# Block 1's FFN: gate and up products with the tokens stationary, their result transposed on TensorE

## The chip, the core and the metric

The kernel runs on one core of one Trainium2 chip. The metric is the device time of one launch in microseconds (us). The profile is of one execution of the same program, taken by the hardware profiler; its times are us from the start of that execution's span, and PE stands for TensorE, DVE for VectorE, ACT for ScalarE, POOL for GpSimd and SP for SyncE.

## What is computed

Two transformer blocks on 256 tokens of width 2048, in float32. Block 1 has a mixer, a cross attention and a gated FFN; block 2 a mixer with pooling and an FFN. The change is in block 1's FFN and in the hand-over to it:

```python
x = x + rms_norm(o @ w_co[l], cross_post_g[l])          # end of the cross attention

h = rms_norm(x, ffn_pre_g[l])
gate, up = jnp.split(h @ w_ffn_in[l], 2, axis=-1)       # 2048 -> 2 x 5632
x = x + rms_norm((jax.nn.silu(gate) * up) @ w_ffn_out[l], ffn_post_g[l])   # 5632 -> 2048
```

`rms_norm` divides each token by the root of its mean square and multiplies by a gain per column.

## The kernel before

**Weights.** All weights come as one stream of halves, 128 x 1024 numbers (512 KB) in the order of use, loaded ahead by SP's queue (L175) into five buffers. Each half is split into `h`, which TensorE takes exactly in a single pass, and the exact rest `l`: ACT copies to `h` (L199), DVE subtracts to `l` (L200; POOL for a few halves). Five buffers hold `h` and `l` of five halves; normally `stream.half()` splits the half that comes four after the one now used. Activations are split in the same way into a `Pair`: for each tile of 128 features the high parts of 256 tokens and then the low parts. A product is `h*H + h*L + l*H`, all three summed in one PSUM accumulator.

**Two forms of product.** `cols` (L349) has the weights stationary: for a tile of 128 weight columns, and each of the 16 k-tiles, one instruction streams the 256 high parts and 256 low parts of the tokens past `h` (512 columns, L379), another the 256 high parts past `l` (L378, for the first k-tile L381). It leaves out^T, features across the partitions, in two halves of a bank that must be added (`sum2`, L475 and L476). `rowsmm` (L397) has the tokens stationary: for 512 weight columns, a token block `tb` of 128 tokens and each k-tile, three instructions of 512 columns (L423 to L425); a half holds two k-tiles, so it takes 12 of these for both token blocks. It leaves tokens across the partitions.

**Accumulators.** `acc()` gives one of three PSUM banks, `bank()` one of five others for transposes and small products.

**Around the products.** Each engine takes its instructions in the order in which the program emits them. `self.later(f)` leaves `f` for the `settle()` after the next half's products; `tick()` runs a step of waiting side work.

**Block 1's FFN** (`ffn`, L1454). The 5632 hidden columns are cut into parts of 8, 8, 8, 8, 4, 8 tiles of 128 (`FFN_PARTS`, 44 tiles). Step `i0` makes part 0 of the hidden values, `o0` multiplies it with its rows of `w_ffn_out`; the order is i0 i1 o0 i2 o1 i3 o2 i4 o3 i5 o4 o5. The i steps use `cols` on tiles of gate and up in turn (32 halves for a part of 8), the o steps `rowsmm` (16 halves). In an i step each tile is added (ACT, DVE), multiplied with `rbx` (L1472), which is 1/rms of each token laid out along the free axis, the same in every partition; a gate tile goes through Silu (L1474), an up tile is multiplied with it (L1477) and split into the Pair `hid` (L468, L469). In o0 the result is copied by ACT (L1490), in o1 to o4 added by DVE (L1492).

**The hand-over.** The cross attention's output product is a `rowsmm` with a chain: its last seven halves run for the first token block and then for the second. Meanwhile the first block's x is updated (`up`, L1180), transposed on TensorE (`tr`, L1218) and split times a gain into the Pair `hT` (`ev`, L1229 on ACT, L1231 on DVE); the last four tiles of `ev` are left for later. After the second token block `after1` makes that block's scale (L1154 and L508 to L512), updates x, has PE run five products of nothing (`warm`, L634), finishes two postponed products with the gain (`finish`, L817), and lays the remaining updates, transposes and splits of the second block, two tiles at a time, between the k-tiles of the first tile of `i0` (`self.pre`). Three halves of weights are split ahead. `stats_gen` makes 1/rms of x and `rbx` beside the next products; the first evictions wait for it.

Of the kernel before, what the change touches and what calls it, by code (L numbers as in the profile page):

```python
# [15 lines left out]
AF = mybir.ActivationFunctionType  # L16
# [25 lines left out]
# ---------------------------------------------------------------- host layout  # L42

def _cols(w):
    """K x N -> per tile of 128 columns, [128 (k in tile), K/128, 128]; K 2048 or 1024."""
    k, n = w.shape
    t = w.reshape(k // 128, 128, n // 128, 128).transpose(2, 1, 0, 3)
    if k == 1024:
        t = t.reshape(n // 256, 2, 128, 8, 128).transpose(0, 2, 1, 3, 4)
    return t.reshape(-1, 128, 2048)  # L50


def _rows(w, n0=0, n1=None):
    """K x N -> per block of 512 columns and 512 rows, [128 (k in tile), 4, 512]."""
    k, n = w.shape
    t = w.reshape(k // 512, 4, 128, n // 512, 512).transpose(3, 0, 2, 1, 4)
    return t.reshape(-1, 128, 2048)


def _weights(a):  # L60
# [13 lines left out]
    gate_up = np.stack([_cols(w_fi[:, :FFN]), _cols(w_fi[:, FFN:])], axis=1).reshape(-1, 128, 2048)  # L74
    starts = np.cumsum((0,) + FFN_PARTS)
    for step in FFN_ORDER:
        p = int(step[1:])
        lo, hi = int(starts[p]), int(starts[p + 1])
        u.append(gate_up[2 * lo:2 * hi] if step[0] == "i" else _rows(w_fo[lo * 128:hi * 128]))
# [70 lines left out]
# ---------------------------------------------------------------- the program  # L150

class Stream:
    """The weights in the order of use, in halves of 128 x 1024: loaded ahead and split into a part
    that the tensor engine's single pass carries exactly and the exact remainder."""
# [14 lines left out]
    def loading(self):  # L169
        """the load of the next half; the very first one in two pieces."""  # L170
# [43 lines left out]
class Pair:  # L214
    """An operand [128 (k in tile), nkt, 256 tokens], split into two parts side by side; 4 k-tiles per slot."""
# [18 lines left out]
class Chain:  # L234
    """What rowsmm does besides: before all of it, after[tb] after the first and the second block of tokens,
    at[i] before the last but i half of the second; the weights that come next are split ahead of the
    second block (ahead) and after its halves in splits."""
# [6 lines left out]
class Prog:  # L244
# [22 lines left out]
    # -- tiles  # L267
# [32 lines left out]
    # -- work that runs beside the products  # L300
    def tick(self):
        """one step of each waiting piece of work, as far as the vector engine has time beside a unit of
        weights; what a generator yields is the cost of its next step there."""
# [33 lines left out]
    def finish(self):  # L337
        """what ev_post leaves for after the start of the chain."""
        last, self.last = self.last, []
        for f in last:  # L340
            f()
# [6 lines left out]
    # -- products  # L348
    def cols(self, xp, nkt, ntiles, evac, ready=None, wide=0, wider=False):  # L349
        """out^T tile j [128 columns, 256 tokens] for each tile of weight columns; with wider, in two halves  # L350
        of a bank that evac has to add (the second: what the low parts of xp give). The first tiles
        (wide) go through the first half of k together. What evac needs may not be there yet: then
        up to four tiles wait until it is (ready)."""
# [42 lines left out]

    def rowsmm(self, xp, nkt, ncb, evac, chain=None, lead=7):  # L397
        """out [128 tokens, 512 columns] for each block of columns and of tokens. With a chain, the last
        halves (lead) are done for the first block of tokens before the second, so that what
        follows the first (chain) runs beside the second."""  # L400
# [35 lines left out]
        for i in range(n):  # L436
# [28 lines left out]
    # -- small pieces  # L465
    def split2(self, v, h, l):
        """h + l = v exactly, h in the tensor engine's single-pass form."""
# [3 lines left out]
    def sum2(self, out, ps):  # L471
        """the two halves that cols leaves."""
# [10 lines left out]
    def split_later(self, v, h, l):  # L483
        """split2, left for after the next products' weights: neither engine waits for the other then."""
# [6 lines left out]
    def rsqrt(self, v, n, scale, eps, y=None):  # L491
        """1 / sqrt(v * scale + eps) of a small tile: the scalar engine's root, inverted, and a Newton step."""
# [11 lines left out]
    def rsqrt2(self, v, scale, eps, name="r"):  # L504
        """rsqrt of [128, 1], in fewer steps."""
# [14 lines left out]
    def diag(self, r):  # L520
        """[128 tokens, 2] on the diagonals of two blocks."""
# [5 lines left out]
    def across(self, d, name="rbc"):  # L527
        """diag of r [128 tokens, 2] -> r [128, 256 tokens], the same in every partition."""
# [8 lines left out]
    def row(self, i, name="row"):  # L537
        """row i of the per-column vectors, the same in every partition."""
# [9 lines left out]
    # -- the whole  # L548
# [81 lines left out]
    def warm(self, n):  # L630
        """n products of nothing, for the tensor engine's clock not to drop while it waits."""
# [4 lines left out]
    def norm_gen(self, t, r):  # L636
        """per token: 1 / sqrt(mean square + eps)."""
# [11 lines left out]
    def small_gen(self):  # L649
        """what depends on the small inputs alone."""  # L650
# [8 lines left out]
        # the lower bound of the forget gate: softmax over one layer, its running sum less the first  # L659
# [13 lines left out]
        # the factor of the second softmax map, negated  # L673
# [10 lines left out]
    def bias_gen(self):  # L684
        """bias[q, h, k] of the distance 128 + q - k, with the causal mask."""
# [35 lines left out]
    # ------------------------------------------------------------ block 1: mixer  # L721
# [79 lines left out]
    def ev_post(self, y, g, ss, add=True):  # L801
        """the last part of a product before a post-norm: the sum, its mean square, times the gain."""
# [21 lines left out]
    def da_gen(self, q, k, v, o_pair):  # L824
# [4 lines left out]
        # per head and map: the second block of queries (256 keys), then the first (128)  # L829
# [81 lines left out]
    def head_out(self, o_t, ss, p, g, gate=None):  # L911
        """o [128 tokens, 2, 8 heads, 128]: its rms norm per head (and gate), transposed, times g, split."""
# [24 lines left out]
    def hg_gen(self, fg, qg, rb):  # L937
# [57 lines left out]
        def s0(i):  # L995
# [4 lines left out]
            if lv == 1:  # L1000
                # q * k for the diagonal; one step back the decay is f = 1 - k itself
# [148 lines left out]
    # ------------------------------------------------------------ post-norm, residual, next operand  # L1150
    def rms_of(self, ss, tb):
        """ss [128, 2, 4] of squares -> 1 / sqrt(mean + eps) of one block of tokens."""
# [4 lines left out]
    def moments(self, c, tb, n):  # L1157
        """of x[tb], n columns from c on, for ln_of."""
# [3 lines left out]
    def ln_of(self, tb):  # L1162
        """of one block of tokens: rsqrt(var + eps), the mean, what sets the last, and -mean * rsqrt."""
# [6 lines left out]
    def residual(self, y, ss):  # L1170
        """update for spread: x += y * rsqrt(mean square)."""
# [12 lines left out]
    def layer(self, g, b):  # L1184
        """update for spread: x = (x - mean) * rsqrt(var + eps) * g + b."""
# [22 lines left out]
    def spread(self, update, xp, g=None):  # L1208
        """the pieces of: update x, then xp = the split of x^T * g; for n tiles of 128 columns from k on of
        the block of tokens tb."""  # L1210
# [10 lines left out]
        def ev(tb, k, n):  # L1221
# [5 lines left out]
            # a bank is read by one engine at a time  # L1227
# [8 lines left out]
    def root(self):  # L1236
        """has the scalar engine ready for its root."""
        self.nc.scalar.activation(out=self.junk[:, :1], in_=self.eps[RMS_EPS], func=AF.Sqrt)

    def chain(self, pieces, order, ahead=3, late=False, stats=None):  # L1240
        """for rowsmm: x and xp, of the first block of tokens beside the products of the second, and of
        the second as the next products (cols) go through k."""
# [47 lines left out]
        return Chain(self.root, after0, after1, {i: at(ks) for i, ks in order.items()}, ahead=ahead)  # L1290
# [478 lines left out]
```

## Time and profile before

| | us |
|---|---|
| median of 3 runs | 2638.34 (2636.83 to 2640.91) |
| span of the profiled execution | 2643.8 |
| PE busy in it | 2606.6 |
| DVE busy | 1706.0 |
| ACT busy | 1306.5 |

Busy time of PE is the time in which at least one instruction is under way; they are pipelined, so that the durations of single ones add up to more than the time. The pace of a stream of products is therefore read from the distance of their starts. "Idle before" in a row is the time that the engine stood still ahead of the instruction, and the name behind the arrow is what ended it. The granted clock of TensorE is given as a share of 2.4 GHz.

### The profile page before, as it was taken

The page shows a single profiled execution, that of the slowest core. Times are in us where ns is not written, and L with a number is a line of the kernel's source. Part 1 is how long each engine was busy: PE and PEld are TensorE (multiplying, and loading weights), DVE is VectorE, ACT ScalarE, POOL GpSimd, SP SyncE. Part 2 cuts the span into 40 slices and gives each one's busy share as a digit, 9 for nine tenths or more (in the row PEclk, how much of TensorE's full clock was granted, in tenths as well). Part 3 has the DMA queues.
Part 4 walks back from the last instruction along what each step waited for, and adds up shares of the span by engine and source line. Part 5 has one row for each costly group of instructions (what it writes and reads, how often), then busy time and mean ns, then how long its engine had stood idle before and what let it go on. Part 6 is the DMA issues. An engine that isn't in the chain of part 4 may idle for free. (4 is left out here: it accounts for less than half of the span.)

```text
span 2643.8 us, 37315 instructions
## 1 busy us (share of the span) xinstructions
PE 2606.6 (99%) x14419; PEld 2254.9 (85%) x14422; DVE 1706.0 (65%) x2416; ACT 1306.5 (49%) x1931; POOL 64.7 (2%) x60
## 2 busy tenths in 40 slices
PE   9999999999999999999999999999999999999997
PEld 8989888988888888888878888888788888888886
DVE  5865757767665656556676765577675665665566
ACT  6533666665454444444444455555454444444443
POOL 0000000110000000000010000000100000000001
PEclk9999999999999999999999999999999999999999
DMA  7544557545555555555556645666455555556553
GB/s 278 179 148 138 177 177 247 197 160 172 186 188 188 189 186 190 192 191 191 184 168 196 215 162 173 191 217 193 148 191 189 186 190 192 190 190 220 191 190 118
DMA packets 134098, 493.57 MB, mean 187 GB/s; under 512 B 15149, under 2 KB 15541, under 8 KB 131744
## 3 DMA queue, kind: packets, MB, share of 16 engines
q1 hardware_dynamic: 129888, 470.34, 54.0%
q0 software_dynamic: 2880, 17.76, 2.0%
q10 hardware_dynamic: 1152, 3.07, 0.3%
q8 instruction: 114, 1.87, 0.3%
q14 instruction: 64, 0.52, 0.1%
HBM read 486.91 MB, written 2.11 MB: 185 GB/s over the span
## 5 line engine op out<-in xcount | busy, mean ns | idle before, releaser
L200 DVE TENSOR_TENSOR l<-w,h 128x1024 fp32r<-128x1024 f32 (+1 forms) x880 | 1071.5, 1223 | 672.7 <-ACT h L199 667.8
L199 ACT ACTIVATE h<-w 128x1024 fp32r<-128x1024 f32 (+1 forms) x883 | 926.4, 1056 | 595.2 <-PE pa L425 381.4
L379 PE MATMUL pa<-hT,h 128*128 128x512 f32 x2376 | 829.9, 398 | 0.0
L378 PE MATMUL pa<-hT,l 128*128 128x256 f32 x2228 | 626.3, 281 | 0.0
L379 PEld LDWEIGHTS pa<-hT,h 128*128 128x128 f32 x2376 | 437.5, 188 | 97.8
L378 PEld LDWEIGHTS pa<-hT,l 128*128 128x128 f32 x2228 | 421.1, 189 | 5.7
L423 PE MATMUL pa<-h,hid 128*128 128x512 f32 (+1 forms) x864 | 334.6, 387 | 0.0
L424 PE MATMUL pa<-l,hid 128*128 128x512 f32 (+1 forms) x864 | 334.4, 387 | 0.0
L425 PE MATMUL pa<-h,hid 128*128 128x512 f32 (+1 forms) x864 | 334.4, 387 | 0.0
L379 PE MATMUL pa<-xT,h 128*128 128x512 f32 x872 | 303.8, 397 | 0.0
L475 ACT ACTIVATE sum<-pa 128x256 f32<-128x256 f32 x239 | 92.1, 386 | 358.4 <-PE pa L379 358.2
L378 PE MATMUL pa<-xT,l 128*128 128x256 f32 x818 | 231.2, 283 | 0.0
L424 PEld LDWEIGHTS pa<-l,hid 128*128 128x128 f32 x864 | 162.2, 188 | 33.2
L425 PEld LDWEIGHTS pa<-h,hid 128*128 128x128 f32 x864 | 162.2, 188 | 33.1
L423 PEld LDWEIGHTS pa<-h,hid 128*128 128x128 f32 x864 | 162.3, 188 | 32.7
L379 PEld LDWEIGHTS pa<-xT,h 128*128 128x128 f32 x872 | 160.2, 188 | 34.8
L476 DVE TENSOR_TENSOR sum<-pa,sum 128x256 f32<-128x256 f32 x183 | 77.8, 425 | 137.1 <-ACT sum L475 137.1
L378 PEld LDWEIGHTS pa<-xT,l 128*128 128x128 f32 x818 | 154.5, 189 | 2.4
L383 PE MATMUL pa<-xT,h 128*128 128x256 f32 x496 | 144.4, 291 | 1.4 <-ACT xT L488 1.4
L385 PE MATMUL pa<-xT,l 128*128 128x256 f32 x496 | 142.5, 287 | 0.2 <-DVE l L200 0.2
L384 PE MATMUL pa<-xT,h 128*128 128x256 f32 x496 | 142.5, 287 | 0.1
L423 PE MATMUL pa<-h,xT 128*128 128x512 f32 x256 | 104.2, 407 | 2.6 <-ACT ghg L738 1.4
(449 smaller groups left out, 3186.1 us busy)
## 6 DMA issues: line engine op xcount, KB each, us to landing
w<-W SPq DMA_DIRECT2D x889, 512.0 KB, 3.9
row<-rows POOLq DMA_DIRECT2D x7, 1024.0 KB, 6.4
xn<-x ACTq DMA_DIRECT2D x2, 1024.0 KB, 10.3
mn<-mem POOLq DMA_DIRECT2D x2, 1024.0 KB, 7.2
memraw<-memT POOLq DMA_DIRECT2D x2, 1024.0 KB, 6.7
x<-x POOLq DMA_DIRECT2D x2, 1024.0 KB, 7.4
xraw<-xT SPq DMA_DIRECT2D x3, 512.0 KB, 9.5
out<-x SPq DMA_DIRECT2D x6, 256.0 KB, 2.5
```

Of the source, the lines that this page charges most:

```text
L199: nc.scalar.activation(out=h[:, s], in_=t[:, s], func=AF.Copy)
L200: (nc.gpsimd if j in self.slow else nc.vector).tensor_tensor(l[:, s], t[:, s], h[:, s].bitcast(F32), OP.subtract)
L378: mm(o[:, :S], l[:, k], xp.H(kt), start=False, stop=False)
L379: mm(o, h[:, k], xp.both(kt), start=kt == 0, stop=kt == nkt - 1)
L383: mm(o, h[:, k], xp.H(kt), start=kt == 0, stop=False)
L384: mm(o, h[:, k], xp.L(kt), start=False, stop=False)
L385: mm(o, l[:, k], xp.H(kt), start=False, stop=kt == nkt - 1)
L423: mm(o, xh, h[:, k, c], start=kt == 0, stop=False)
L424: mm(o, xh, l[:, k, c], start=False, stop=False)
L425: mm(o, xl, h[:, k, c], start=False, stop=kt == nkt - 1)
L475: nc.scalar.activation(out=t, in_=ps[:, S:], func=AF.Copy)
L476: nc.vector.tensor_tensor(t if out is None else out, ps[:, :S], t, OP.add)
```

## The change

The i steps of block 1's FFN use `rowsmm`: tokens stationary, 512 gate columns and then the 512 up columns that go with them, which the host lays out in that order. `ev_glu` takes each accumulator with one instruction: Silu of gate times r on ACT, and (up times r) times that on DVE; r, 1/rms per token, is now a scalar per partition, so `rbx` isn't made. The product has tokens across the partitions, so `turn_later` transposes it on TensorE, four tiles of 128 x 128 to a bank, after the next half's products for the first token block and after the one behind that for the second; the split into `hid` reads that bank one half later.

In the hand-over (`lagged`) the warm-up products are gone, the second block's x is updated and transposed four tiles at a time, and `rowsmm` of i0 (`lag=4`) runs its first four halves for the first token block alone and then for the second, with the second block's pieces between them. Halves 3 to 5 are split while the first block's products run, ahead of these pieces in the queues of ACT and DVE.

```diff
-    gate_up = np.stack([_cols(w_fi[:, :FFN]), _cols(w_fi[:, FFN:])], axis=1).reshape(-1, 128, 2048)
+    gate_up = np.stack([_rows(w_fi[:, i:i + FFN]).reshape(-1, 4, 128, 2048) for i in (0, FFN)], axis=1)
...
-        u.append(gate_up[2 * lo:2 * hi] if step[0] == "i" else _rows(w_fo[lo * 128:hi * 128]))
+        u.append(gate_up[lo // 4:hi // 4].reshape(-1, 128, 2048) if step[0] == "i" else _rows(w_fo[lo * 128:hi * 128]))
...
-    def rowsmm(self, xp, nkt, ncb, evac, chain=None, lead=7):
+    def rowsmm(self, xp, nkt, ncb, evac, chain=None, lead=7, lag=0):
...
-        for i in range(n):
+        first = []
+        for tb in range(2 if lag else 0):
+            for i in range(lag):
+                if tb == 0:
+                    first.append(view(stream.half(2)))
+                self.pre.pop((tb, i), lambda: None)()
+                run(*halves[i], first[i], tb)
+                if tb and i % 2:
+                    stream.split()
+                    self.tick()
+        assert not self.pre or not lag
+        for i in range(lag, n):
...
-    def chain(self, pieces, order, ahead=3, late=False, stats=None):
+    def chain(self, pieces, order, ahead=3, late=False, stats=None, lagged=False):
...
-        return Chain(self.root, after0, after1, {i: at(ks) for i, ks in order.items()}, ahead=ahead)
+        def piece(k, more=None):
+            def f():
+                tr(1, k, 4)
+                ev(1, k, 4)
+                if more is not None:
+                    up(1, more, 4)
+                if more == 12 and stats is not None:
+                    self.stats = self.start(self.norm_gen(self.x, stats))
+            return f
+
+        def after1_lagged():
+            prep(1)
+            up(1, 0, 4)
+            up(1, 4, 4)
+            self.finish()
+            if late:
+                ev(0, 12, 4)
+            self.pre = {(0, 2): piece(0, 8), (0, 3): piece(4, 12), (1, 1): piece(8), (1, 3): piece(12)}
+
+        return Chain(self.root, after0, after1_lagged if lagged else after1, {i: at(ks) for i, ks in order.items()}, ahead=ahead)
...
-        self.rowsmm(o_pair, 4, 4, self.ev_post(y, g, ss, add=False), self.chain(self.spread(self.residual(y, ss), self.hT, self.ffn_pre), ORDER, late=True, stats=self.rxx))
+        self.rowsmm(o_pair, 4, 4, self.ev_post(y, g, ss, add=False), self.chain(self.spread(self.residual(y, ss), self.hT, self.ffn_pre), ORDER, late=True, stats=self.rxx, lagged=True))
...
-
-                def ev(j, ps, hp=hid[p]):
-                    t = self.sum2(None, ps)
-                    nc.vector.tensor_tensor(t, t, self.rbx, OP.mult)
-                    if j % 2 == 0:
-                        nc.scalar.activation(out=t, in_=t, func=AF.Silu)
-                        sg[0] = t
-                    else:
-                        nc.vector.tensor_tensor(t, t, sg[0], OP.mult)
-                        self.split_later(t, hp.H(j // 2), hp.L(j // 2))
-
-                self.cols(hT, 16, 2 * nt, ev, self.have_rbx, wider=True)
+                self.rowsmm(hT, 16, nt // 2, self.ev_glu(hid[p]), lag=4 if p == 0 else 0)
...
+    def ev_glu(self, hp):
...
+        def f(c0, tb, ps):
+            r = self.rxx[:, tb:tb + 1]
+            blk, up = divmod(c0 // 512, 2)
+            if not up:
+                self.drain(self.stats)
+                sg[tb] = self.t2([128, 512], "sg")
+                nc.scalar.activation(out=sg[tb], in_=ps, func=AF.Silu, scale=r)
+                return
+            t = sg.pop(tb)
+            nc.vector.scalar_tensor_tensor(out=t, in0=ps, scalar=r, in1=t, op0=OP.mult, op1=OP.mult)
+            self.turn_later(t, hp, 4 * blk, tb)
+        return f
+
+    def turn_later(self, t, hp, k, tb):
...
+        def tr():
+            ps = self.bank()
+            for i in range(4):
+                self.nc.tensor.transpose(ps[:, i * 128:(i + 1) * 128], t[:, i * 128:(i + 1) * 128], self.ident)
+            self.later(lambda: self.split2(
+                ps.rearrange("p (k t) -> p k t", k=4), hp.H(k, 4, tb * 128, tb * 128 + 128), hp.L(k, 4, tb * 128, tb * 128 + 128)))
+
+        def wait():
+            self.later(tr)
+        self.later(wait if tb else tr)
```

## Rows read from the trace of the kernel before

**Rows 1.** The page: span, busy time by engine, and the weights' split on ACT.

```profile
span 2643.8 us, 37315 instructions
PE 2606.6 (99%) x14419; PEld 2254.9 (85%) x14422; DVE 1706.0 (65%) x2416; ACT 1306.5 (49%) x1931; POOL 64.7 (2%) x60
...
L199 ACT ACTIVATE h<-w 128x1024 fp32r<-128x1024 f32 (+1 forms) x883 | 926.4, 1056 | 595.2 <-PE pa L425 381.4
```

**Rows 2.** Busy time by stretch: engines, then granted clock, DMA share, GB/s.

```profile
580.00:590.00 10.00, 10.00 (x65) 8.91 (x63) 9.46 (x28) 5.81 (x21) 2.84 (x2) 1.00 0.58 217
590.00:595.00 5.00, 2.30 (x11) 0.87 (x10) 3.92 (x16) 4.29 (x17) 0.00 (x0) 1.00 0.01 2
595.00:598.40 3.40, 3.35 (x11) 2.80 (x12) 2.14 (x8) 0.62 (x2) 0.00 (x0) 0.50 0.00 0
598.40:607.00 8.60, 8.22 (x48) 6.56 (x47) 5.39 (x16) 6.36 (x17) 0.00 (x0) 1.00 0.01 2
607.00:780.00 173.00, 173.00 (x985) 150.43 (x984) 115.91 (x166) 91.08 (x136) 0.00 (x0) 1.00 0.59 192
```

**Rows 3.** What PE waited for, 590 to 1350 us: total, times, longest.

```profile
PE pa L634 <- ACT junk L518: 3.5, 2, 2.8
PE pa L379 <- DVE hT L1231: 1.8, 2, 1.5
```

**Rows 4.** Timeline of PE: first products of o0, i2, o1, i3, o2.

```profile
780.16 0.39 PE L423 MATMUL pa<-h,hid 128*128 128x512 f32 x1
...
823.68 0.39 PE L379 MATMUL pa<-hT,h 128*128 128x512 f32 x1
...
914.02 0.39 PE L423 MATMUL pa<-h,hid 128*128 128x512 f32 x1
...
957.54 0.39 PE L379 MATMUL pa<-hT,h 128*128 128x512 f32 x1
...
1047.89 0.39 PE L423 MATMUL pa<-h,hid 128*128 128x512 f32 x1
```

**Rows 5.** Timeline of PE: transposes between products; then all transposes of their line.

```profile
584.10 0.60 PE L1218 MATMUL pb<-ident,x 128*128 128x128 f32 x4
584.46 0.48 PE L423 MATMUL pa<-h,ocx 128*128 128x512 f32 x1
584.77 0.40 PE L424 MATMUL pa<-l,ocx 128*128 128x512 f32 x1
...
L1218 PE MATMUL pb<-ident,x x128: 270/273/447, 487.6 to 1921.2; 128*128 128x128 f32 x128
```

**Rows 6.** Timeline of DVE at the end of o2; ACT's evictions in o0.

```profile
1089.98 1.23 DVE L200 TENSOR_TENSOR l<-w,h 128x1024 fp32r<-128x1024 f32 x1 [1.49 <-ACT h L199]
1091.12 1.28 DVE L1492 TENSOR_TENSOR yf<-pa,yf 128x512 f32<-128x512 f32 x2
...
L1490 ACT ACTIVATE yf<-pa x8: 598/599/601, 789.9 to 823.9; 128x512 f32<-128x512 f32 x8
```

**Rows 7.** Timeline of PE: the last product of the cross attention.

```profile
589.99 0.28 PE L425 MATMUL pb<-h,ocx 128*128 128x256 f32 x1
```

**Rows 8.** Timeline of DVE and ACT in the hand-over.

```profile
581.51 3.34 DVE L1180 SCALAR_TENSOR_TENSOR x<-yc,r,x 128x512 f32<-128x512 f32 x4
...
587.95 2.16 DVE L1231 SCALAR_TENSOR_TENSOR hT<-pb,pv,hT 128x128 fp32r<-128x128 f32 x8 [0.22 <-ACT hT L1229]
...
591.27 1.12 ACT L1229 ACTIVATE hT<-pb,pv 128x128 fp32r<-128x128 f32 x4
...
591.90 0.21 DVE L512 TENSOR_SCALAR r<-d,r 128x1 f32<-128x1 f32 x1
...
592.95 0.42 DVE L817 TENSOR_TENSOR yc<-pa,row 128x256 f32<-128x256 f32 x1
...
593.28 0.42 DVE L817 TENSOR_TENSOR yc<-pb,row 128x256 f32<-128x256 f32 x1
...
606.10 4.63 DVE L200 TENSOR_TENSOR l<-w,h 128x1024 fp32r<-128x1024 f32 x4 [1.71 <-ACT h L199]
```

More of the change, by code (lines that the diff above doesn't have):

```diff
@@ L1459, in ffn @@
         hid = {}
-        sg = {}
         g = self.row(2)
@@ L1493, in ffn @@
             self.rowsmm(hid.pop(p), nt, 4, ev)
+    def ev_glu(self, hp):
+        nc = self.nc
+        sg = {}
+        def f(c0, tb, ps):
[20 more added lines that the diff above has]
+        self.later(wait if tb else tr)
     def rope_gen(self, cs):
```

## The prediction

> **What bounds the kernel now.** I read the page's busy table first: TensorE (PE) is busy 2606.6 us of a span of 2643.8 us, DVE 1706.0 us [rows 1]. Then the stretches around block 1's FFN: from 607 to 780 us PE is busy 173.00 of 173.00 us, DVE 115.91 and ACT 91.08, at clock 1.00 [rows 2]. In such a stretch only two things move the time: the pace of PE's own instructions, and a new wait in front of one of them. The exception is the hand-over from the cross attention's output product to the FFN, 590 to 607 us: PE is busy 2.30 of the first 5.00 us, and the 3.4 us after that run at clock 0.50, the lower level of 1.2 GHz, behind the idle time [rows 2]. The waits name what PE waits for there: the squares on ACT whose output the warm-up products read, and the low parts of the second token block on DVE [rows 3]. So I cost three terms: the pace of a half of weights, the new transposes, the hand-over. Whatever shrinks on DVE or ACT inside the FFN is worth nothing by itself.
>
> **Term 1, the pace.** FFN steps i and o alternate, and the first PE instruction of each gives its length [rows 4]. Step i2 runs from 823.68 to 914.02 us, 90.34 us for its 32 halves, 2.823 us each; i3 (957.54 to 1047.89) gives 90.35 us, the same. Steps o0 (780.16 to 823.68) and o1 (914.02 to 957.54) take 43.52 us for 16 halves, 2.720 us each. Both kinds stream the same number of columns per half, 8 x (512 + 256) = 12 x 512 = 6144; the i form does it in 16 instructions, half of them narrow, the o form in 12. The change turns every i half into the o form: the same instruction, 128 tokens stationary and 512 weight columns moving, with hT in the place of hid. FFN_PARTS sums to 44 tiles of hidden columns, twice that for gate and up, two halves each: 176 halves. Gain: 176 x (2.823 - 2.720) = 18.1 us. The order of weights in memory changes, the number of halves, their bytes and their split into h and l do not, so DMA, ACT and DVE pay per half what they pay now.
>
> **Term 2, the transposes.** Eleven blocks of 512 hidden columns, two token blocks each, four transposes of 128x128: 22 groups, 88 instructions, all on PE and so all on the path. The nearest rows are the same transposes between products of the same width: the group at 584.10 us starts the next product at 584.46 and the one after at 584.77 [rows 5]. Without the group the second of these products would have started one product's spacing (2.720 / 12 = 0.227 us) after 584.10; so the group costs 584.77 - 584.10 - 0.227 = 0.443 us, 0.11 us per transpose. (Two more groups in that product, of 8 and of 4, work out to the same 0.11.) Loss: 22 x 0.443 = 9.7 us. Bounds: 0.36 us per group if the following product lost nothing, 7.9 us in all; 4 x 0.273 = 1.09 us if nothing overlapped and each took the full duration of its row [rows 5], 24.0 us in all. I take the spacing, because instructions of PE overlap: the 512-column product has a duration of 0.39 us and a spacing of 0.227.
>
> The Trainium skill (TensorE: Matmul & The Clock Gate, Part 4: PE-mode transpose) gives about 275 ns for a transpose inside a kernel and says that transposes do not count as activity for the clock. The first figure is the duration of the row, not its spacing; by it the sum would be near zero, and that is a rival below. On the second, no row speaks against a full clock: the 10 us with those transposes have clock 1.00 [rows 2].
>
> **Who could make PE wait inside a step.** After the last half of an up block DVE multiplies each token block out of PSUM with the activated gate (new 512-column instruction, nearest row the o-step's eviction at 1091.12 us, 1.28 us for two [rows 6]); the first group of transposes stands behind one more half of products, the second behind two. Counted from the start of that last half, ACT and DVE first split the half that comes four later (ACT 1.06 [rows 1], DVE 1.23 [rows 6]), so DVE is free at about 2.5 us and done with the first block by 3.2 and the second by 3.9; the transposes come at 5.4 and 8.6 us. That is 2 us of cover. The rows agree: DVE's evictions begin at 1091.12 us, right behind its split at 1089.98, with nothing between [rows 6]. On the gate side ACT takes 0.60 us per block [rows 6]; there are three accumulators and each block of columns needs two, so the second token block of the next columns waits for the first block's gate to be out: freed at about 2.2 us, wanted at 4.1. Steps o0 and o1 have the same accumulators, evictions of the same size on ACT and on DVE, twice as often per half, and show no loss. Queued behind these instructions are the next splits, which have a lead of four halves. I cost these waits at 0 inside the steps.
>
> **What is removed besides.** Per tile an ACT copy and two DVE passes of 256 columns, the row of r across the partitions (two small products, one DVE copy), five warm-up products. All of it lies beside PE except the warm-ups and the small products, which are inside the hand-over that I measure as a whole.
>
> **Term 3, the hand-over.** Now: the last product of cross attention starts at 589.99 us [rows 7], so PE could go on at 590.11. Steps i0 and i1 end at 780.16 [rows 4]: 190.05 us, less 64 x 2.823 = 180.7, leaves 9.4 us, its 16 transposes included. After: the first four halves run on the first token block alone, whose parts for k-tiles 4 to 11 are made by 590.1 [rows 8] and those before them earlier; PE need not wait at 590.11. Then it depends on DVE, which I follow by its rows [rows 8]: the scale is ready at 592.11 (591.90 + 0.21); each 512-column update of x 0.84 (592.95, 593.8), the two postponed products with the gain 0.75 (594.5), low parts of the first block's last four tiles 1.1 (595.6), the splits of halves 3 and 4, which the change moves in front, 1.16 each (596.8, 598.0), low parts of the second block's tiles 0 to 3 (599.1), update 8 (599.9), split 5 (601.1), low parts 4 to 7 (602.2), update 12 (603.05), low parts 8 to 11 (604.2), split 6 (605.3), low parts 12 to 15 (606.4). ACT does its share (1.12 per four tiles [rows 8], 1.06 per half) ahead of DVE each time. PE at 1.36 us per half and token block and 0.44 per group: two halves to 592.8; first group, waiting for x to 592.95, to 593.4; third half 594.75; second group 595.2; fourth half waits for its l at 596.8, to 597.9; first half of the second block waits for low parts, to 599.5; third group waits for update 8, to 600.35; 601.7, 603.05; fourth group 603.5; last of the eight at 604.85. That is 14.7 us, less 4 x 2.720, so 3.9 us lost, and perhaps 0.5 more for the hand-overs themselves: 4.4. Gain 9.4 - 4.4 = 5.0 us. Bounds: 7.6 us gained if DVE were never late (only the transposes' 1.78 are left); 0 if its waits add up to 3 us more and the clock falls again for 3.4 us (1.7 us lost, as at 595.00 to 598.40 [rows 2]). I take 5.0, as PE's longest wait in this walk is 1.5 us where it now is nearly idle for 5. The splits that move forward also start five weight loads on SP's queue some 10 us earlier; DMA is at 0.00 to 0.01 there [rows 2], so nothing is pushed back. The squares for r come beside products and are wanted only at about 615 us.
>
> **Sum.** 18.1 - 9.7 + 5.0 = 13.4 us. The profiled execution's span of 2643.8 would become 2630.4; it stands 0.2% above the median of the runs, 2638.34, from which I predict 2624.9, say 2625.0 us.
>
> **Rivals.** (a) The hand-over gains nothing: DVE, now with splits in its chain, is late at each of five hand-overs and the clock falls. Speaks for it: nearly all steps on DVE's list end within 1 us of PE's need. Against: PE has products to run in between. Result 18.1 - 9.7 = 8.4 us gained, 2629.9 us. Chance 0.12. (b) A transpose costs its full duration: 18.1 - 24.0 + 5.0 = -0.9, that is 2639 us, no change. For it: durations; against it: three groups whose spacing was read. The Trainium skill's 275 ns would give the same. Chance 0.06. (c) The slower side: PE takes its instructions in order, so a group of transposes whose multiplication is not done stops all products behind it. Cover is 2 us; if DVE came later than that, by a split waiting for weights or for its buffer, each of the 22 groups would stall by the excess. From 0.6 us per group the whole gain is gone, from 0.85 us it is slower by 5 us; at 1 us it is 2638.3 - 13.4 + 22 = 2647 us. Against it: the evictions on DVE at 1091.12 us [rows 6] run on time. Chance 0.04. (d) The change does all that it says, the forecast: 0.78.
>
> **How the numbers follow.** A measurement of this kernel tells about 0.2%, 5.3 us, from no change, so faster means under 2633.1 us: the forecast nearly whole and (a), 0.88; within 0.2% is (b) and the tail of (a), 0.08; slower is (c), 0.04. The range: the low end 18.1 - 7.9 + 7.6 = 17.8 us gained, 2620.5, and 2 us for the spread of the runs (2636.83 to 2640.91): 2618.5. The high end takes in (a) with a group dearer by 0.1 us (2.2) and the same spread: 2634.
>
> **What would show it.** Right: inside steps i2 and i3 products 0.227 us apart and PE without idle time. A step of 32 halves has 4 blocks of columns, so 2 blocks of hidden columns and 4 groups of transposes: 32 x 2.720 + 4 x 0.443 = 88.8 us in place of 90.3. The way from 590.1 us to the end of i1 shrinks from 190.05 to about 182 us: 64 x 2.720 + 8 x 0.443 + 4.4, of which up to two groups may fall into o0. Wrong: PE idle ahead of a transpose with DVE as the releaser (c), a group that sets the next product back by about 1.1 us (b), clock 0.50 after 590 us or waits of PE there of over 3 us in one piece (a).

## The result

The changed kernel takes 2624.53 us (2622.58 to 2632.06), the kernel before 2639.47 us beside it; the ratio is 0.9948 (0.9934 to 0.9963). The forecast was 2625.0 us.

The page of the changed kernel, span and busy time by engine, against [rows 1]:

```profile
span 2622.5 us, 35624 instructions
PE 2589.1 (99%) x13797; PEld 2220.4 (85%) x13797; DVE 1628.0 (62%) x2189; ACT 1270.2 (48%) x1799; POOL 64.6 (2%) x60
```

PE has 622 instructions less and is busy 17.5 us less; its share of the span is what it was. DVE's 78 us less are not in the time.

The spans differ by 21.3 us, the medians by 14.9, so the two profiled executions must be compared stage by stage and not as a whole. The last product of the cross attention starts at 589.99 us before [rows 7] and at 584.20 now: 5.8 us were lost before the changed part begins, in code that is the same. From there to the last product of block 1's FFN, a stretch that I call the FFN stretch from here on, it is 748.92 us (589.99 to 1338.91) before and 735.32 us (584.20 to 1319.52) now: 13.6 us. The remaining 1.9 us come behind it. The last product of the FFN in PE's timeline of before:

```profile
1338.91 0.28 PE L425 MATMUL pb<-h,hid 128*128 128x256 f32 x1
```

Busy time by stretch (engines PE, PEld, DVE, ACT, POOL, then granted clock, DMA share, GB/s) shows what the two differences outside are. Of before:

```profile
200.00:300.00 100.00, 100.00 (x682) 90.16 (x681) 65.86 (x113) 44.00 (x80) 0.00 (x0) 0.97 0.44 140
...
1342.50:1345.30 2.80, 2.04 (x8) 0.69 (x6) 2.54 (x8) 0.77 (x2) 0.00 (x0) 0.51 0.15 60
1345.30:1357.70 12.40, 12.40 (x62) 10.41 (x63) 8.14 (x17) 6.04 (x11) 0.00 (x0) 0.84 0.08 22
```

Of after, at the same places of the program:

```profile
200.00:300.00 100.00, 100.00 (x704) 89.46 (x702) 70.16 (x122) 45.07 (x84) 0.00 (x0) 1.00 0.44 144
...
1322.40:1325.80 3.40, 3.07 (x9) 1.35 (x9) 2.75 (x10) 0.98 (x3) 0.00 (x0) 0.51 0.35 135
1326.00:1336.60 10.60, 10.60 (x61) 8.83 (x62) 8.04 (x17) 5.94 (x11) 0.00 (x0) 1.00 0.08 30
```

From 200 to 300 us the clock was granted at 0.97 in one execution and at 1.00 in the other, in code that the change doesn't touch. The other rows are the hand-over out of block 1's FFN, also untouched, and the first tile of the next stage. There the clock fell in both, but before it was still low in that tile (0.84), which took 12.4 us, and in the changed kernel it was back at 1.00 for the same work, which took 10.6 us. This is chance of the execution and no part of the change.

**Inside the steps.** The first products of o0, i2, o1 and i3 in the timeline of PE after, against [rows 4], and the last product of the FFN:

```profile
764.66 0.39 PE L424 MATMUL pa<-h,hid 128*128 128x512 f32 x1
...
809.13 0.39 PE L424 MATMUL pa<-h,hT 128*128 128x512 f32 x1
...
897.13 0.39 PE L424 MATMUL pa<-h,hid 128*128 128x512 f32 x1
...
941.60 0.39 PE L424 MATMUL pa<-h,hT 128*128 128x512 f32 x1
...
1319.52 0.28 PE L426 MATMUL pb<-h,hid 128*128 128x256 f32 x1
```

Step i2 takes 88.00 us in place of 90.34, o0 and o1 take 44.47 in place of 43.52, since two of an i step's four groups of transposes come behind its last block, in the o step. A pair of o and i is 132.47 us where it was 133.86: 1.39 us gained. One group in the timeline, against [rows 5]:

```profile
633.97 0.60 PE L1539 MATMUL pb<-ident,sg 128*128 128x128 f32 x4
634.32 0.48 PE L424 MATMUL pa<-h,hT 128*128 128x512 f32 x1
634.63 0.40 PE L425 MATMUL pa<-l,hT 128*128 128x512 f32 x1
```

634.63 - 633.97 - 0.227 = 0.433 us set back, 0.443 in the row of before.

**The hand-over.** PE's timeline after: the last product of cross attention, the first of i0, the longest wait, and the first product of the fifth half:

```profile
584.20 0.28 PE L426 MATMUL pb<-h,ocx 128*128 128x256 f32 x1
584.32 0.40 PE L424 MATMUL pa<-hl,hT 128*128 128x512 f32 x1
...
590.67 0.50 PE L425 MATMUL pa<-l,hT 128*128 128x512 f32 x1 [0.79 <-DVE l L200]
...
598.60 0.39 PE L424 MATMUL pa<-h,hT 128*128 128x512 f32 x1
```

PE goes from one stage into the other without a gap, and four halves with 16 transposes take 598.60 - 584.32 = 14.28 us, 3.4 more than 4 x 2.720. Busy time by stretch after, against [rows 2]:

```profile
584.30:587.70 3.40, 3.40 (x19) 2.62 (x18) 2.32 (x9) 2.93 (x10) 0.00 (x0) 1.00 0.04 13
587.70:591.10 3.40, 2.62 (x15) 1.96 (x14) 3.40 (x9) 3.40 (x10) 0.00 (x0) 1.00 0.00 0
591.10:598.60 7.50, 7.46 (x38) 5.87 (x36) 7.35 (x17) 6.12 (x20) 0.00 (x0) 1.00 0.66 212
```

All that PE waited for from 584 us to the first product of block 2's mixer at 1325.97, against [rows 3] (total, times, longest):

```profile
PE pa L646 <- ACT junk L530: 2.5, 1, 2.5
PE pa L425 <- DVE l L200: 0.8, 1, 0.8
PE pb L1230 <- DVE x L1192: 0.7, 1, 0.7
PE pa L379 <- DVE xT L481: 0.5, 1, 0.5
```

The clock stays at 1.00. Of the four waits only the second, of 0.79 us, is in this hand-over; the other three lie from 1315 us on in the next one, out of block 1's FFN, which the change leaves alone. No wait at all lies inside the i steps and the o steps before that.

### The profile page after: what moved, and what is told of

It is laid out like the page before. It is cut to its first block, busy times and chain, and to the rows that moved or that the text cites. A ratio compares the mean times of both kernels' runs of the same rounds, so it can differ in the third digit from the quotient of the medians.

```text
span 2622.5 us, 35624 instructions
## 1 busy us (share of the span) xinstructions
PE 2589.1 (99%) x13797; PEld 2220.4 (85%) x13797; DVE 1628.0 (62%) x2189; ACT 1270.2 (48%) x1799; POOL 64.6 (2%) x60
## 5 line engine op out<-in xcount | busy, mean ns | idle before, releaser
L379 PE MATMUL pa<-hT,h 128*128 128x512 f32 x1008 | 352.4, 398 | 0.0
L424 PE MATMUL pa<-h,hT 128*128 128x512 f32 x692 | 270.6, 391 | 0.0
L425 PE MATMUL pa<-l,hT 128*128 128x512 f32 x692 | 269.3, 389 | 0.8 <-DVE l L200 0.8
L426 PE MATMUL pa<-h,hT 128*128 128x512 f32 x692 | 269.4, 389 | 0.0
L378 PE MATMUL pa<-hT,l 128*128 128x256 f32 x945 | 265.7, 281 | 0.0
L378 PE MATMUL pa<-xT,l 128*128 128x256 f32 x818 | 231.2, 283 | 0.0
L379 PEld LDWEIGHTS pa<-hT,h 128*128 128x128 f32 x1008 | 185.7, 188 | 41.5
L378 PEld LDWEIGHTS pa<-hT,l 128*128 128x128 f32 x945 | 178.6, 189 | 2.4
L487 ACT ACTIVATE sum<-pa 128x256 f32<-128x256 f32 x152 | 58.7, 386 | 219.7 <-PE pa L379 219.2
L425 PEld LDWEIGHTS pa<-l,hT 128*128 128x128 f32 x692 | 130.0, 188 | 27.7 <-DVE l L200 1.1
L426 PEld LDWEIGHTS pa<-h,hT 128*128 128x128 f32 x692 | 129.9, 188 | 27.1
```

The source lines that it names most:

```text
L378: mm(o[:, :S], l[:, k], xp.H(kt), start=False, stop=False)
L379: mm(o, h[:, k], xp.both(kt), start=kt == 0, stop=kt == nkt - 1)
L424: mm(o, xh, h[:, k, c], start=kt == 0, stop=False)
L425: mm(o, xh, l[:, k, c], start=False, stop=False)
L426: mm(o, xl, h[:, k, c], start=False, stop=kt == nkt - 1)
L487: nc.scalar.activation(out=t, in_=ps[:, S:], func=AF.Copy)
```

## The experiments

Each starts from the changed kernel unless it is said otherwise. The ratio is to the kernel before (the changed kernel: 0.9948), measured beside it. The last two columns come from the profiled execution: the FFN stretch, and its difference from that of the changed kernel. The stretch is free of what the clock does elsewhere: in the seven executions in which block 1's FFN and the hand-over to it are those of the changed kernel it is 735.32 to 735.34 us. So it tells fractions of a microsecond that the medians don't.

| kernel | median us | ratio (95%) | FFN stretch us | against after |
|---|---|---|---|---|
| before | 2639.47 | 1 | 748.92 | +13.60 |
| after | 2624.53 | 0.9948 (0.9934 to 0.9963) | 735.32 | 0 |
| no_turn | 2618.49 | 0.9914 (0.9896 to 0.9931) | 724.77 | -10.55 |
| double_turn | 2634.77 | 0.9985 (0.9975 to 0.9994) | 744.50 | +9.18 |
| turn_now | 2635.22 | 0.9981 (0.9972 to 0.9991) | 743.67 | +8.35 |
| no_lag | 2633.99 | 0.9981 (0.9970 to 0.9991) | 742.12 | +6.80 |
| old_handover | 2631.90 | 0.9975 (0.9966 to 0.9985) | 741.25 | +5.93 |
| ff2_rows | 2629.21 | 0.9955 (0.9937 to 0.9972) | 735.34 | +0.02 |
| ff2_lag | 2621.62 | 0.9935 (0.9920 to 0.9950) | 735.33 | +0.01 |
| u_lag | 2625.62 | 0.9949 (0.9934 to 0.9964) | 735.33 | +0.01 |
| u_late | 2622.82 | 0.9945 (0.9932 to 0.9959) | 735.33 | +0.01 |
| ff2_late | 2618.77 | 0.9927 (0.9914 to 0.9939) | 735.32 | 0 |
| both_late | 2619.74 | 0.9925 (0.9913 to 0.9937) | 735.33 | +0.01 |

### What the transposes cost: no_turn and double_turn

```diff
             ps = self.bank()
-            for i in range(4):
-                self.nc.tensor.transpose(ps[:, i * 128:(i + 1) * 128], t[:, i * 128:(i + 1) * 128], self.ident)
-            self.later(lambda: self.split2(ps.rearrange(...), ...))
+            self.later(lambda: self.split2(t.rearrange(...), ...))      # no_turn
...
-            for i in range(4):
+            for i in (0, 1, 2, 3) * 2:                                  # double_turn
                 self.nc.tensor.transpose(...)
```

> The changed kernel (2624.5 us) without its 88 transposes: hid is split straight from the untransposed product, so the values of block 1's FFN are wrong, every other instruction and its place stay. Theory (a group of four costs PE its spacing, 0.44 to 0.47 us): 22 groups less, 9.7 to 10.3 us faster, about 2614.5 us; step i2 87.1 us in place of 88.0. Rival (each transpose costs its full duration of 0.27 us): 24 us faster, 2600 us. Rival (transposes hide in gaps between products): no change.

> Every group of transposes is issued twice into the same bank. Theory: eight in a row cost 0.80 + 0.08 us in place of 0.36 + 0.08, so 22 x 0.44 = 9.7 us slower than the changed kernel, 2634 us. Rival (full duration, 4 x 0.27 = 1.09 us more per group): 24 us slower, 2648.5 us. Rival (transposes do not count as activity and the clock falls): more than either, with a granted clock under 1.00 in the FFN.

Without them the FFN stretch is 10.55 us shorter, 0.48 us per group of four; a pair of o and i is 130.57 us, so (132.47 - 130.57) / 4 = 0.475 us per group. Both are a little above the 0.443 read from one group, as the dozen products behind the first group of a block stand 0.23 us apart and only then 0.227 again. The median fell by less, 6.0 us, in four runs that spread over 8.5 us; the stretch is the sharper measure. Twice the transposes add 9.18 us, 0.42 per group. A group in the timeline of double_turn:

```profile
633.78 1.03 PE L1539 MATMUL pb<-ident,sg 128*128 128x128 f32 x8
634.57 0.48 PE L424 MATMUL pa<-h,hT 128*128 128x512 f32 x1
634.89 0.40 PE L425 MATMUL pa<-l,hT 128*128 128x512 f32 x1
```

634.89 - 633.78 - 0.227 = 0.88 us for eight. Rival (b), the full duration, would have asked for 24 us both ways; it is out. So is the clock: busy time by stretch in double_turn has 1.00 with 176 transposes.

```profile
766.00:1100.00 334.00, 334.00 (x1516) 277.54 (x1515) 168.87 (x156) 140.74 (x146) 0.00 (x0) 1.00 0.57 188
```

The Trainium skill (TensorE: Matmul & The Clock Gate, Part 4: PE-mode transpose) says that transposes don't count as activity for the clock. No run here shows that or speaks against it: the two groups of a block stand 3.2 us apart, and at least 41 us of products come before the next two.

no_turn also shows the pace alone. The products of one line in i2 of no_turn (count, durations in ns, first and last start):

```profile
L424 PE MATMUL pa<-h,hT x128: 389/389/389, 808.5 to 894.8; 128*128 128x512 f32 x128
```

127 distances of three products in 86.3 us are 0.2265 us per product, with hT stationary as with hid. 130.57 us for 48 halves are 2.720 us each: the first term stands to the last digit.

### What hides the multiplication on DVE: turn_now

```diff
-        def wait():
-            self.later(tr)
-        self.later(wait if tb else tr)
+        tr()
```

> The transposes stand right behind the last half of the up block in PE's queue in place of one and two halves later. Theory (cover by one half of products is what hides the multiplication on DVE): PE waits about 0.5 us ahead of the first group of each block and 0.3 to 0.5 ahead of the second, 0.8 to 1.0 us x 11 blocks = 9 to 11 us slower than the changed kernel, about 2634.5 us, DVE named as the releaser of the transposes. Rival (PE's queue or DVE's speed hides it without the delay): 2624.5 us and no wait.

The FFN stretch is 8.35 us longer, 0.76 us per block of 512 hidden columns. The first block in PE's timeline, and what PE waited for from 600 to 1340 us:

```profile
634.23 1.32 PE L1539 MATMUL pb<-ident,sg 128*128 128x128 f32 x8 [0.35 <-DVE sg L1530]
```

```profile
PE pb L1539 <- DVE sg L1530: 3.9, 11, 0.4
```

PE stands idle for 0.35 us ahead of the first group, in each of the 11 blocks (0.51 us counted by starts, as the product in front starts at 633.49), and loses another 0.3 between the two groups, since the eight take 1.32 us and not the 1.03 of double_turn. This is rival (c) made to happen: same instructions, other places in PE's queue, and more than half of the gain is gone. The expected 0.8 to 1.0 us per block was a little high.

### What the hand-over is worth: no_lag and old_handover

```diff
-            self.pre = {(0, 2): piece(0, 8), (0, 3): piece(4, 12), (1, 1): piece(8), (1, 3): piece(12)}
+            for f in (piece(0, 8), piece(4, 12), piece(8), piece(12)):
+                f()
...
-                self.rowsmm(hT, 16, nt // 2, self.ev_glu(hid[p]), lag=4 if p == 0 else 0)
+                self.rowsmm(hT, 16, nt // 2, self.ev_glu(hid[p]), lag=0)      # no_lag
```

> The hand-over to block 1's FFN with all pieces of the second token block in front of i0, and i0 without its first four halves for the first token block alone; no warm-up products, four tiles at a time, as in the changed kernel. Theory (the gain of the hand-over is that PE has products that need only the first token block): PE stands until the last update of x is transposed, about 9 us after the cross attention's last product, where the changed kernel loses 3.4 us in all: 5.7 us slower than the changed kernel, 2630 us, up to 2633 if the clock falls. Rival (the gain came from dropping the warm-up products and from pieces of four tiles): within 1.5 us of the changed kernel, 2625 us.

The FFN stretch is 6.80 us longer; 5.7 were expected, and up to 8.5 with a fallen clock, as it is here. All of it comes before o0 (187.24 us from the last cross product to o0, 180.46 in after). Busy time by stretch of no_lag, whose last cross product starts at 582.69, and what PE waited for there:

```profile
582.80:587.80 5.00, 1.48 (x10) 0.83 (x8) 3.92 (x14) 3.27 (x14) 0.00 (x0) 0.91 0.01 2
587.80:592.20 4.40, 1.91 (x9) 1.51 (x9) 3.71 (x12) 3.21 (x11) 0.00 (x0) 0.50 0.00 0
592.20:596.00 3.80, 3.80 (x16) 3.08 (x15) 3.24 (x10) 3.44 (x8) 0.00 (x0) 0.80 0.02 4
```

```profile
PE pb L1230 <- DVE x L1192: 6.0, 3, 2.7
```

PE stands 6 us for the updates of x, and the clock falls in the course of it; by the granted clock of the three rows that costs up to 3.4 us. With those taken off, 3.4 us still stand between this kernel and the changed one, more than the 1.5 that the rival allows, so it falls: pieces of four tiles and no warm-up products are not where the gain comes from. Whether they save anything by themselves, with a clock that holds, isn't shown.

old_handover keeps i0 as it was (weights stationary, 16 tiles, `rbx`) with the old `after1`, and only i1 to i5 in the new form:

```diff
+                if p == 0:
...
+                    self.cols(hT, 16, 2 * nt, ev, self.have_rbx, wider=True)      # ev, weights' order and after1 as before
+                    continue
                 self.rowsmm(hT, 16, nt // 2, self.ev_glu(hid[p]))
```

> The changed kernel with the old hand-over and the old form (weights stationary) in i0 alone; i1 to i5 tokens stationary with transposes. Theory (the hand-over is worth 6 us, and per 32 halves the pace gains 3.3 and four groups of transposes take 1.9): 7.4 us slower than the changed kernel, 2632 us; the way from the last cross product to the end of i1 about 188.7 us. Rival (the whole gain is in the steps i1 to i5): 2626 us.

The median comes out 7.4 us above the changed kernel's, the FFN stretch 5.93 us. From 582.87 us (last cross product 582.75) to o0 at 769.10 are 186.23 us; less 32 x 2.823, 32 x 2.720 and two groups of 0.475 that leaves 7.9 us for the old hand-over, where 9.4 were read from before. The stretch behind the idle time tells the difference, against the 0.50 of [rows 2]:

```profile
582.80:587.80 5.00, 2.32 (x11) 0.84 (x10) 3.92 (x16) 4.24 (x16) 0.00 (x0) 1.00 0.03 11
587.80:591.20 3.40, 3.33 (x20) 2.83 (x21) 3.03 (x11) 1.25 (x4) 0.00 (x0) 1.00 0.00 0
```

The same 5 us with 2.3 us of PE's work, and this time the clock didn't fall; in before it did for 3.4 us, half of which is 1.7. So the lag is worth 7.9 - 3.4 = 4.5 us, and 6.0 us in an execution in which the old hand-over loses the clock.

### Does the form pay without a gate: ff2_rows

Block 2's FFN has no gate: each product of 512 columns must be transposed, where block 1's FFN transposes one of two.

```diff
+                if p > 0:
+                    def ev_rows(c0, tb, ps, hp=hid[p]):
+                        t = self.t2([128, 512], "sq")
+                        nc.scalar.activation(out=t, in_=ps, func=AF.Relu)
+                        nc.vector.tensor_tensor(t, t, ps, OP.mult)
+                        self.turn_later(t, hp, c0 // 128, tb)
+                    self.rowsmm(hT, 16, nt // 4, ev_rows)
+                    continue
                 self.cols(hT, 16, nt, ev, wider=True)
```

> On top of the changed kernel, block 2's FFN steps i1 to i7 also with tokens stationary and their result transposed; no gate there, so each product of 512 columns is transposed, not each second one. Theory: 112 halves x 0.103 = 11.5 us gained by the pace, 28 groups x 0.47 = 13.2 us lost, so 1.6 us slower than the changed kernel, 2626 us. Rival (the form gains by itself, the transposes are cheap): 2613 us. Rival (a group costs 1.09 us): 2643.5 us.

The ratio is 0.9955, 0.0007 above the changed kernel's, 1.8 us, far within its interval. The profile is sharper: from the last product of block 2's mixer to the last of its FFN it is 721.24 us in after and 722.59 us here, 1.35 us longer; in the seven executions whose code from block 2's mixer on is that of after, this stretch lies between 720.87 and 721.28 us. The form gains 8 x 0.103 = 0.82 us per 512 weight columns, and the two groups of a hidden block cost 0.95 us. With gate and up sharing them 1.65 us are gained for 0.95 lost; without a gate it is 0.82 for 0.95.

### Does the lag pay elsewhere: ff2_lag, u_lag, and their second versions

```diff
+                if p == 0:                                   # ff2_lag: step i0 of block 2's FFN alone, ev_rows as in ff2_rows
...
+                    self.rowsmm(hT, 16, nt // 4, ev_rows, lag=4)     # chain(..., ahead=2, lagged=True)
+                    continue
                 self.cols(hT, 16, nt, ev, wider=True)
...
-        self.cols(xT, 16, 8, ev_to(u), wider=True)           # u_lag: first product of block 2's mixer
+        self.rowsmm(xT, 16, 2, ev_u, lag=4)                  # ev_u: ACT copies, PE transposes, ACT copies; chain(..., lagged=True)
```

> On top of the changed kernel, block 2's FFN step i0 alone with tokens stationary and its hand-over lagged in the same way (four halves for the first token block, then for the second). Theory (the idle time in a hand-over is filled by work on the first token block): PE now stands about 5 us there and runs at a lower clock behind it, about 10 us lost in all; DVE's work on the second block (a layer norm with gain and bias) ends about 14 us after the last product, so about 3.5 us stay lost: 6 us faster, less 0.2 for i0's transposes, 2618.5 us. Rival (DVE's longer chain sets this hand-over, lag or not): 2624.5 us.

> On top of the changed kernel, the hand-over from block 1's FFN to block 2's mixer lagged in the same way: its first product u with tokens stationary, transposed by four groups and copied by ACT. Theory: about 6 us idle before the first product and a slow start behind it now; with the lag 4 to 6 us faster, 2619.5 us. Rival (the side work that starts there on DVE, the angles of the rotation, delays the pieces): 2624.5 us.

ff2_lag gains 2.5 us from the last product of block 2's mixer to o0 (99.30 us, 101.85 in after) where 6 were expected; u_lag gains 0.3 us from the last product of block 1's FFN to the mixer's fourth product, v, (143.77, 144.07 in after), nothing that a median tells. What PE waited for in the two places, ff2_lag and then u_lag:

```profile
PE pb L1230 <- DVE x L1217: 2.4, 1, 2.4
PE pa L425 <- DVE l L200: 1.4, 1, 1.4
```

```profile
PE pb L1230 <- DVE x L1192: 2.7, 2, 2.0
PE pa L424 <- ACT ur L1633: 2.1, 1, 2.1
```

In both, the two halves in front of the first piece end before DVE has the second block's x, PE idles for some 2 us and the clock falls (0.56 from 1895 to 1900 us in ff2_lag); in u_lag the sine of the rotation's angles then stands on ACT in front of u's first eviction. The second versions go at these causes:

```diff
         def after1_lagged():
+            for _ in range(early):                           # 1 in u_late, 2 in ff2_late
+                self.stream.slow.add(self.stream.ns)
+                self.stream.split()
             prep(1)
...
+            if early:
+                self.pre = {(0, 3): piece(0, 8), (1, 0): piece(4, 12), (1, 2): piece(8), (1, 3): piece(12)}
...
-        self.start(rp)                                       # u_late: the angles after u
```

> As u_lag, with three edits at its waits: one more half of weights split ahead of the scale (its subtraction on POOL), the second block's pieces one half later (PE does three halves of the first block before it wants x), and the angles of the rotation begun after u. Theory (u_lag gained nothing because PE waited 1.96 us for x, ran 3.4 us at a lower clock behind that, and later waited 2.1 us for ACT, where the sine of the angles stood in front of u's eviction): these 4 to 5 us come free, 2620 us. Rival (DVE sets the hand-over whatever the order): 2624.5 us.

> As ff2_lag, with two more halves split ahead of the scale (their subtraction on POOL) and the second block's pieces one half later. Theory (ff2_lag still lost 2.4 us waiting for x, 1.4 for a split on DVE and 2.5 us by the clock): 2 to 4 us faster than ff2_lag, 2618.5 us. Rival (DVE's chain of layer norm and splits sets it): as ff2_lag, 2621.5 us.

> u_late and ff2_late together, on top of the changed kernel: two hand-overs 1.3 ms of program apart in places of their own, so the two gains add: 2624.5 - 4.5 - 6 = 2614 us. Rival (each of them gains only by the phase of the clock): 2620 to 2624 us.

ff2_late takes 96.82 us to o0, 5.0 less than after; u_late 141.83 us to v, 2.2 less, and not the 4 to 5 expected; both_late 96.94 and 141.71, so the two add to 7.3 us. In the medians ff2_late is 0.9927 and both_late 0.9925: the fastest kernel of this study by ratio that keeps the transposes, though the 2 us of u_late can't be told in whole programs. both_late's median, 2619.74, misses the 2614 expected and lies just below the 2620 to 2624 of its rival, the phase of the clock. The stretches speak against that rival for ff2_late: in block 2's hand-over the clock is at 0.50 for 3.4 us in both_late as it is in after, and both_late is 4.9 us shorter. For u_late they leave the clock a part: no_turn, with the hand-over as in after and a clock that held in it, takes 143.63 us to v, so 1.8 us of the 2.2 are u_late's own.

The waits for x are not gone, they are no shorter than in the first versions (2.7 us in ff2_late, 2.5 in u_late); but PE has done one half more ahead of them, and the clock is at 1.00 behind them in both. What PE waited for in u_late (the shorter of the two waits for x lies ahead of the hand-over), and busy time by stretch:

```profile
PE pb L1230 <- DVE x L1192: 3.2, 2, 2.5
PE pa L426 <- DVE xT L481: 1.2, 1, 1.2
```

```profile
1325.00:1331.00 6.00, 3.22 (x17) 2.50 (x18) 6.00 (x8) 2.65 (x4) 2.98 (x5) 1.00 0.53 144
```

DVE is busy 6.00 of 6.00 us there: now its chain sets the hand-over, as the rival had it. More halves for the first block alone would be the next thing to try; that wasn't done.

## Why the prediction was right

**Term 1** was exact: 2.720 us per half in i steps (no_turn), 18.1 us in all. Why 16 instructions took 2.823 us for the same columns, no run shows.

**Term 2** was 9.7 us; removing the transposes gives 10.55 us back, 10.5 by the pairs of steps. The step that was too small is the price per group, read as 0.443 us from the first two products behind it; the products after those are still slightly apart, and 0.475 is what a group costs. Reading the distance to the product after next was right in kind, but not far enough. The choice of the spacing, and not the duration of 0.273 us, was right.

**The waits inside a step** were costed at nothing, with 2 us of cover by the delay of one half. PE's list of waits has none there, and turn_now shows what they cost without that cover: 0.76 us per block.

**Term 3** was 5.0 us, and is 9.4 - 3.4 = 6.0 between the two profiled executions. The walk along DVE's queue had the order and the waiting right: after the scale at 586.34 us (592.11 in the walk, 5.8 us earlier as all of this execution) the splits of halves 3 and 4 begin at 589.40 (595.6 - 5.8 = 589.8), and the last of the eight half-blocks ends at 598.60 (604.85 - 5.8 = 599.05).

```profile
586.37 1.42 DVE L1192 SCALAR_TENSOR_TENSOR x<-yc,r,x 128x512 f32<-128x512 f32 x2
...
589.40 2.35 DVE L200 TENSOR_TENSOR l<-w,h 128x1024 fp32r<-128x1024 f32 x2
```

The updates of x took 0.71 us each and not 0.84, and the splits began 0.4 us sooner; the longest wait is 1.0 us by starts (590.67 - 589.41 - 0.227; 0.8 of it is idle time in the profile), where the walk had 1.5. The 0.5 us put on top for the hand-overs themselves didn't appear. Part of the 9.4 us that were taken as the price of the old hand-over was the clock of that one execution, 1.5 us, as old_handover shows; the prediction did not say that its start value could vary.

**Rivals.** (a) didn't come: the clock stays at 1.00 and the longest wait is 0.8 us. (b) is out by two experiments. (c) is real as a mechanism and absent in this kernel. What the prediction named as marks came out: the way to the end of i1 is 180.34 us (584.32 to 764.66; about 182 was said), products 0.227 us apart, no idle time inside a step. The way is below 182 as two groups lie in o0 and the hand-over lost 3.4 us, not 4.4. Step i2 is 88.0 and not 88.8 us only because two of its groups lie in o1, where they make up the difference.

**The sum:** 18.1 - 10.5 + 6.0 = 13.6 us, 13.6 measured in the FFN stretch, 13.4 predicted. That the two agree to 0.2 us is luck: two errors of about 1 us, in transposes and hand-over, had opposite signs, and 1.5 of the 6.0 us are the clock of the one execution before; with the old hand-over's 7.9 us it is 12.1. That the median came within 0.5 us of 2625.0 is luck as well, as the four runs of the changed kernel spread over 9.5 us. What was right by its mechanism are the three terms, their signs and the absence of waits inside a step.

## What to carry to other kernels

On an engine that is busy all the time, cost an edit by the distance between starts, over enough instructions to see the pace return, and not by durations; then ask only which new wait stands at the head of its queue and what runs in front of it. A transposition that two products share pays for a faster form, one that each product needs for itself doesn't (1.35 us slower here). And a hand-over between stages can be filled by the half of the data that is ready, but only as far as the chain on the other engine is shorter than the filler: the same edit gave 4.5 to 6.0 us in one place, 2.5 in another and 0.3 in a third.

## What was not expected of the hardware

The same idle time doesn't always cost the clock, and a fallen clock doesn't always cost the same. The hand-over with 2.3 us of PE's work in 5 us was followed by 3.4 us at 0.50 in before [rows 2] and by 1.00 in old_handover, where it took 1.5 us less. The next one, out of block 1's FFN, has the same code in ten of the executions. From the FFN's last product to v it takes 143.63 us in no_turn, where the clock holds; 143.99 to 144.10 us in the five with 3.4 us at 0.50, in after under warm-up products, transposes and idle time; and 145.59 to 145.89 us in the four with 6.8 us at 0.50, in before more than half of it under the products of the next stage. In both_late 3.4 us at 0.50 made 0.1 us, against ff2_late:

```profile
1891.00:1894.40 3.40, 3.40 (x12) 2.56 (x11) 3.40 (x5) 2.19 (x5) 0.00 (x0) 0.50 0.32 73
```

PE is busy all the time there, but what it does at half the clock ends before DVE has the next data: a wait of 1.2 us for the low parts of hT, which ff2_late has behind these products, is missing in both_late. So a fallen clock costs only as far as PE's own work sets the pace, 0.1 to 2.3 us here, and no number of one execution should carry it as a constant.
